# Solving the inverse's 16 by 16 diagonal blocks one to a partition, by way of DRAM

## The chip, the core and the metric

The kernel runs on one core of a Trainium2 chip. Its time is device microseconds of one execution, lower is better; a comparison takes the median of several runs on the same chip. Engines are named as in the profile: PE (TensorE matmul), PEld (its weight loads), DVE (VectorE), ACT (ScalarE), POOL (GpSimd), SP (SyncE, which here issues nearly all DMAs). All data are float32.

## What is computed

One layer of a hybrid backbone over 2048 latent tokens and 256 context tokens, 1024 channels wide. After an adaptive LayerNorm and one wide projection with w_in, branch A is a bidirectional gated delta rule with 8 heads of 128 channels, branch B a gated short convolution; both are projected, merged, projected again and added to the residual. The part that matters here is branch A's scan in chunks. With keys k, decays and write strengths beta of a chunk, the reference does

```python
m = jnp.where(tri_strict, jnp.einsum('bhncd,bhnsd->bhncs', k_beta, k) * decay, 0.0)
t_inv = lax.linalg.triangular_solve(eye + m, jnp.broadcast_to(eye, m.shape), left_side=True, lower=True)
u = t_inv @ v_beta; w = t_inv @ (k_beta * exp(g_cum))      # then, chunk after chunk:
v_new = u - w @ s; o = q_dec @ s + qk @ v_new; s = s * d + k_dec^T @ v_new
```

so each chunk, direction and head needs the inverse of a unit triangular matrix. The kernel uses chunks of 128 tokens, hence 18 chunks (16 latent, 2 context), and 128 by 128 inverses.

## The kernel before

It has three stages: the input projections (to about 1840 us of the profile), the scan with products of the two branches beside it (to about 2950 us), and the rest of those products with the output projection. In the projections, one small load (L1066) brings the 32 logit columns of w_in to 128 partitions, 8 pieces of 32 float32 (128 bytes) to a partition, 1024 pieces in all.

The scan makes 36 *visits*: 18 chunks, each for the two directions d = 0 and d = 1 in turn. A visit of all 8 heads passes through a software pipeline of four steps, so that in an iteration of the loop in `window` four visits are worked on: `v3` (the newest: loads, decays, N), `v2` (the product of queries and keys), `v1` (inverse) and `v0` (the recurrence with the state S). The order of PE's instructions is written out by hand; between them, `dense(n)` puts single matrix passes of the branch products (`pf`, L1227 to L1231), 24 in most iterations. The order on the other engines and on SP's DMA queue is made by the framework's scheduler from its own estimate of times, and at run time each of them is a queue that stands when its first instruction waits.

- `visit_decay` (L126 on) makes the decays between positions, `gcb`, on DVE (L140, eight instructions) and ACT.
- `gram` (L158 to L167) multiplies the keys of a chunk into `N`, [128, 8 heads, 128]. At the first of the two visits to a latent chunk it also keeps the product for the other direction in DRAM (`kkd`, `kqd`, by way of POOL L164); at the second it loads that (L151) and scales it with one DVE instruction (L152).
- `inv_base`, in the same iteration as N, solves the 16 by 16 blocks on N's diagonal. ACT cuts out the 32 by 32 diagonal blocks with their sign changed (`n32`, L177, four instructions); ACT and DVE bring the 16-blocks into `n16` (L180 to L182), where each of 128 partitions holds one row of a block for each head. Then 15 steps of substitution follow, with `R` starting as the identity (POOL, L185). Each has three DVE instructions: a shuffle that sends row i of each block to the other 15 partitions (L191), the product with the column i of n16 (L192), the sum into R (L193):

```python
nc.vector.stream_shuffle(rbv, R[:, :, c0:c1], [i] * 16 + [16 + i] * 16)
nc.vector.tensor_tensor(out=rbv, in0=rbv, in1=bc(n16[:, :, i:i + 1], w), op=ALU.mult)
nc.vector.tensor_tensor(out=R[:, :, c0:c1], in0=R[:, :, c0:c1], in1=rbv, op=ALU.add)
```

  Two ACT instructions (L196) spread R over the 32 columns of `r32`, and a DVE transposition of 32-blocks (L198) makes `r32t`.
- `inv_w16` (L210, copy to `w16` at L213) and `inv_d16` (L222, L224, L226), two iterations later, join 16-blocks to 32-blocks with small matmuls; `inv_w32`, `inv_d32`, `inv_w64`, `inv_d64` go on to 128.
- `st_ks` (L299, L301), `st_v` (L308), `st_o` (L319, L320) and `st_u` (L327, L332) are the recurrence; the output sums go through the callback at L1265 to L1268. The first L299 of an iteration marks its start on PE.

## Time and profile before

| | |
|---|---|
| median of 3 runs | 3305.19 us (3304.52 to 3312.04) |
| span of the profiled execution | 3301.7 us (first to last instruction) |
| PE busy | 3035.6 us, 92% |
| DVE busy | 2283.1 us, 69% |
| ACT, POOL busy | 47%, 49% |
| DMA | 481.75 MB, mean 146 GB/s |

The profile is of one execution, and for it the span is what is given; the time of the runs lies a few microseconds above it. Busy shares are averages over all three stages. Idle time is put down to the instruction that ended it ("<-").

### The profile page before, as it was taken

The numbers are of one execution on the slowest core, as the hardware profiler recorded it, in microseconds if no ns is written. First come the engines' busy times: TensorE is split into PE (matmuls) and PEld (weight loads), VectorE is DVE, ScalarE is ACT, GpSimd is POOL, SyncE is SP. The second block draws the span as 40 slices with busy tenths as digits, with TensorE's granted clock in tenths as the row PEclk, the third lists the DMA queues.
The fourth block names the chain that finished last, engine by engine and source line by source line (L and its number), as shares of the span: only waits on it lengthen the run. The fifth ranks groups of instructions, "written<-read, shape, count | busy, mean of one in ns | idle before, by whom it ended". The sixth has DMA issues, their size and how long they took to land.

```text
span 3301.7 us, 60541 instructions
## 1 busy us (share of the span) xinstructions
PE 3035.6 (92%) x22089; PEld 2484.4 (75%) x22089; DVE 2283.1 (69%) x5815; ACT 1561.9 (47%) x3453; POOL 1628.0 (49%) x1156
## 2 busy tenths in 40 slices
PE   7899999999998999999999888888889888898988
PEld 3677777788886777888878677887777777776766
DVE  7656545555646564555622678899898989978699
ACT  4664633333456555333434355555555665664321
POOL 3444557665576554666666333343343233424464
PEclk9999999999999999999999988889999989999999
DMA  5533322225564432222332654465566667667742
GB/s 210 142 99 96 95 80 87 74 64 156 173 186 136 115 93 76 64 64 65 98 108 86 214 172 150 167 196 170 174 205 212 212 216 239 219 209 241 228 146 102
DMA packets 423047, 481.75 MB, mean 146 GB/s; under 512 B 25428, under 2 KB 324949, under 8 KB 421724
## 3 DMA queue, kind: packets, MB, share of 16 engines
q1 hardware_dynamic: 413646, 470.43, 45.5%
q10 hardware_dynamic: 9102, 7.45, 0.7%
q8 instruction: 173, 2.83, 0.4%
q14 instruction: 126, 1.03, 0.1%
HBM read 341.32 MB, written 136.47 MB: 145 GB/s over the span
## 4 chain that ended last, share of the span: by engine, by line
PE 52%; DVE 25%; issue 6%; ACT 5%; DMA 5%; POOL 3%; SPq 1%; DVEq 0%; ACTq 0%; POOLq 0%
PE pd L743 13%; PE pd L744 13%; PE pd L745 13%; DVE gcb L140 3%; DVE rb L192 3%; DVE R L193 2%; POOL al L352 2%; DVE rb L191 2%; DMA gcb<-gcd 1%; PE pst L319 1%; ACT n L177 1%; POOL s L729 1%; DVE N L167 1%; PE pst L320 1%; DVE t L988 1%
## 5 line engine op out<-in xcount | busy, mean ns | idle before, releaser
L743 PE MATMUL pd<-bh,ah 128*128 128x512 f32 x2240 | 898.0, 401 | 9.8 <-ACT u L763 5.3
L745 PE MATMUL pd<-bh,al 128*128 128x512 f32 x2240 | 886.3, 396 | 0.0
L744 PE MATMUL pd<-bl,ah 128*128 128x512 f32 x2240 | 886.3, 396 | 0.0
L352 POOL TENSOR_TENSOR al<-s,ah 128x512 fp32r<-128x512 f32 x348 | 478.1, 1376 | 427.6 <-ACT ah L351 408.5
L352 POOL TENSOR_TENSOR al<-raw,ah 128x512 fp32r<-128x512 f32 x260 | 372.7, 1436 | 339.4 <-ACT ah L351 296.1
L743 PEld LDWEIGHTS pd<-bh,ah 128*128 128x128 f32 x2240 | 423.5, 189 | 107.2 <-issue 6.4
L745 PEld LDWEIGHTS pd<-bh,al 128*128 128x128 f32 x2240 | 423.5, 189 | 99.7 <-DVE al L352 0.4
L744 PEld LDWEIGHTS pd<-bl,ah 128*128 128x128 f32 x2240 | 424.0, 189 | 94.2
L351 ACT CAST ah<-s 128x512 fp32r<-128x512 f32 x352 | 215.0, 618 | 358.7 <-PE pd L744 342.8
L351 ACT CAST ah<-raw 128x512 fp32r<-128x512 f32 x264 | 162.5, 617 | 263.7 <-PE pd L744 213.8
L729 DVE TENSOR_TENSOR s<-s,raw 128x512 f32<-128x512 f32 x80 | 97.0, 1213 | 218.0 <-POOL s L729 161.5
L1231 PE MATMUL pf<-ah,wl 128*128 128x512 f32 x512 | 221.8, 433 | 6.7 <-DVE wl L352 4.6
L1227 PE MATMUL pf<-ah,wh 128*128 128x512 f32 x512 | 214.2, 419 | 12.4 <-DVE R L193 5.0
L1229 PE MATMUL pf<-al,wh 128*128 128x512 f32 x512 | 214.8, 420 | 5.9 <-POOL al L352 3.0
L352 POOL TENSOR_TENSOR wl<-wraw,wh 128x1024 fp32r<-128x1024 f32 x48 | 115.9, 2416 | 197.5 <-ACT wh L351 66.5
L192 DVE TENSOR_TENSOR rb<-rb,n 128x8 f32<-128x8 f32 (+6 forms) x540 | 200.8, 373 | 5.0
L140 DVE SCALAR_TENSOR_TENSOR gcb<-gcb,gc,mask 128x128 f32<-128x128 f32 x288 | 178.0, 623 | 9.1 <-ACT qd L137 8.1
L138 POOL TENSOR_TENSOR qd<-qd,qT 128x1024 f32<-128x1024 f32 x32 | 76.4, 2386 | 202.8 <-ACT qd L137 199.2
L193 DVE TENSOR_TENSOR R<-R,rb 128x8 f32<-128x8 f32 (+6 forms) x540 | 158.1, 294 | 5.6
L319 PE MATMUL pst<-S,qd 128*128 128x128 f32 x512 | 112.2, 304 | 33.7 <-ACT ot L1265 17.0
L768 DVE TENSOR_TENSOR u<-pd,u 128x512 f32<-128x512 f32 x80 | 55.0, 687 | 116.7 <-PE pd L745 113.6
L1005 ACT ACTIVATE t<-t 128x512 f32<-128x512 f32 (+1 forms) x112 | 67.3, 601 | 141.2 <-DVE t L990 141.2
(346 smaller groups left out, 6242.2 us busy)
## 6 DMA issues: line engine op xcount, KB each, us to landing
raw<-in_w_in SPq DMA_DIRECT2D x160, 512.0 KB, 4.0
kT<-kTd SPq DMA_DIRECT2D x36, 512.0 KB, 5.1
gcb<-gcd SPq DMA_DIRECT2D x36, 512.0 KB, 4.1
kt<-kd SPq DMA_DIRECT2D x36, 512.0 KB, 4.5
vh<-vd SPq DMA_DIRECT2D x36, 512.0 KB, 4.3
wraw<-in_w_b SPq DMA_DIRECT2D x32, 512.0 KB, 5.0
qT<-qTd SPq DMA_DIRECT2D x32, 512.0 KB, 3.9
wraw<-in_w_a SPq DMA_DIRECT2D x32, 512.0 KB, 5.2
```

Source lines behind the costliest of these rows:

```text
L140: nc.vector.scalar_tensor_tensor(out=gcb[:, h, :], in0=gcb[:, h, :], scalar=gcT[:, h:h + 1], in1=self.mask[d], op0=ALU.subtract, op1=ALU.min)
L192: nc.vector.tensor_tensor(out=rbv, in0=rbv, in1=bc(n16[:, :, i:i + 1], w), op=ALU.mult)
L193: nc.vector.tensor_tensor(out=R[:, :, c0:c1], in0=R[:, :, c0:c1], in1=rbv, op=ALU.add)
L319: nc.tensor.matmul(po[:, j, :], v["qd"][:, h, :], S[:, h, :], start=True, stop=False)
L351: self.nc.scalar.copy(out=hi, in_=src)
L352: (eng or self.nc.gpsimd).tensor_tensor(out=lo, in0=src, in1=hi.bitcast(F32), op=ALU.subtract)
L743: mm(ps, hi[:, k, :], bh, start=(first and k == 0), stop=False, skip_group_check=not first)
L744: mm(ps, hi[:, k, :], bl, start=False, stop=False, skip_group_check=not first)
L745: mm(ps, lo[:, k, :], bh, start=False, stop=(last and k == 3), skip_group_check=not first)
L1227: mm(ps, wh[:, k, :], ah, start=(k == 0), stop=False)
L1229: mm(ps, wh[:, k, :], al, start=False, stop=False)
L1231: mm(ps, wl[:, k, :], ah, start=False, stop=(k == KT - 1))
```

## The change

The base of the inverse is split into three functions, and the diagonal blocks change their layout.

- `inv_gather`, where `inv_base` was: four DMAs write N's 32 by 32 diagonal blocks to a DRAM buffer `nd` (one of four in turn), and two DMAs read from it the 16-blocks into `blk`, [64, 16, 16]: one whole block to a partition (8 heads x 8 blocks = 64). Pieces are 128 bytes for the writes and 64 for the reads, 256 and 512 of them to a DMA.
- `inv_solve`, one iteration later, behind the decays of `v3`: POOL sets the middle columns of a standing tile `X` to the identity; for each of 15 rows there is one product of column i of blk with row i of X, both broadcast (at most 64 elements on 64 partitions), and one subtraction. Two DMAs write X with its zero margins to a DRAM buffer `rd` as rows of 32, one DMA reads that back as `r32`; pieces of 128 bytes, 512 and 1024 to a DMA.
- `inv_turn`, at the start of the iteration of `inv_w16`: the DVE transposition from r32 to r32t.
- `inv_w16` takes N's own diagonal blocks, and the sign moves into the copy of `w16`.

All new DMAs are issued by SP. The constants of the old layout go away, and X and an identity are filled once ahead of the scan. (Comments are removed as well, which the diff below leaves out.)

```diff
-        i16 = pool.tile([P, 16], F32, name="i16")
...
-            nc.vector.tensor_scalar(out=t, in0=io, scalar1=idx, scalar2=None, op0=op)
-            self.tri16.append(t)
...
+        self.X = [self.g1.tile([64, 16, 48], F32, name=f"X{i}") for i in range(2)]
+        for x in self.X:
+            self.nc.gpsimd.memset(x, 0.0)
+        self.eye16 = self.g1.tile([64, 16, 16], F32, name="eye16")
+        self.nc.gpsimd.memset(self.eye16, 0.0)
+        self.nc.gpsimd.memset(self.eye16.rearrange("p r c -> p (r c)")[:, 0:256:17], 1.0)
...
-    def inv_base(self, v):
...
+    def inv_gather(self, v):
+        nd, dma = self.nd_d[v["at"] % 4], self.nc.sync.dma_start
         for g in range(4):
             s = slice(32 * g, 32 * g + 32)
-            nc.scalar.mul(out=n32[s], in_=N[s, :, s], mul=-1.0)
...
+            dma(nd[:, s, :].rearrange("h q c -> q h c"), v["N"][s, :, s])
+        v["blk"] = blk = self.g2.tile([64, 16, 16], F32, name="blk")
+        nv = nd.rearrange("h (a b r) (e c) -> (h a) b r e c", b=2, r=16, e=2)
+        for b in range(2):
+            dma(blk[32 * b:32 * b + 32], nv[:, b, :, b, :])
+
+    def inv_solve(self, v):
+        nc, g2, d, blk = self.nc, self.g2, v["d"], v["blk"]
+        v["X"] = X = self.X[v["at"] % 2]
+        nc.gpsimd.tensor_copy(out=X[:, :, 16:32], in_=self.eye16)
         for i in (range(15, 0, -1) if d == 0 else range(0, 15)):
-            c0, c1 = (i, 16) if d == 0 else (0, i + 1)
...
+            rs, cs = (slice(0, i), slice(i, 16)) if d == 0 else (slice(i + 1, 16), slice(0, i + 1))
+            xs = slice(16 + cs.start, 16 + cs.stop)
+            nr, w = rs.stop - rs.start, cs.stop - cs.start
+            pr = g2.tile([64, 64], F32, name="pr")[:, 0:nr * w].rearrange("p (r c) -> p r c", c=w)
+            nc.vector.tensor_tensor(out=pr, in0=blk[:, rs, i:i + 1].to_broadcast([64, nr, w]),
+                                    in1=X[:, i:i + 1, xs].to_broadcast([64, nr, w]), op=ALU.mult)
+            nc.vector.tensor_tensor(out=X[:, rs, xs], in0=X[:, rs, xs], in1=pr, op=ALU.subtract)
         v["r32"] = r32 = g2.tile([P, H, 32], F32, name="r32")
-        for hf in range(2):
-            nc.scalar.mul(out=r32[:, :, 16 * hf:16 * hf + 16], in_=R, mul=self.m16[hf])
-        v["r32t"] = r32t = g2.tile([P, H, 32], F32, name="r32t")
-        nc.vector.transpose(self.fl(r32t), self.fl(r32))
+        rd = self.rd_d[v["at"] % 4]
+        rv = rd.rearrange("h (a b r) c -> (h a) b r c", b=2, r=16)
+        for b in range(2):
+            nc.sync.dma_start(rv[:, b], X[32 * b:32 * b + 32, :, 16 - 16 * b:48 - 16 * b])
+        nc.sync.dma_start(r32, rd.rearrange("h p c -> p h c"))
+
+    def inv_turn(self, v):
+        v["r32t"] = r32t = self.g2.tile([P, H, 32], F32, name="r32t")
+        self.nc.vector.transpose(self.fl(r32t), self.fl(v["r32"]))
...
-                nc.tensor.matmul(wp[s, h, :], v["n32"][s, h, :], v["r32t"][s, h, :], start=True, stop=True)
+                nc.tensor.matmul(wp[s, h, :], v["N"][s, h, s], v["r32t"][s, h, :], start=True, stop=True)
...
-            nc.scalar.copy(out=v["w16"], in_=wp)
+            nc.scalar.mul(out=v["w16"], in_=wp, mul=-1.0)
...
+        self.nd_d = [dt(f"nd{i}", [H, P, 32]) for i in range(4)]
+        self.rd_d = [dt(f"rd{i}", [H, P, 32]) for i in range(4)]
...
                 if v1:
                     self.visit_load2(v1)
+                    self.inv_turn(v1)
                     self.inv_w16(v1)
...
                 if v3:
                     self.visit_decay(v3)
+                if v2:
+                    self.inv_solve(v2)
...
                     self.gram(v3, "N", v3["kT"])
-                    self.inv_base(v3)
+                    self.inv_gather(v3)
```

## Rows read from the trace of the kernel before

**Rows 1.** The page: span; busy time of each engine; DMA queue q1.

```profile
span 3301.7 us, 60541 instructions
...
PE 3035.6 (92%) x22089; PEld 2484.4 (75%) x22089; DVE 2283.1 (69%) x5815; ACT 1561.9 (47%) x3453; POOL 1628.0 (49%) x1156
...
q1 hardware_dynamic: 413646, 470.43, 45.5%
```

**Rows 2.** Windows: projections, scan, two single visits; columns in the first line.

```profile
core 0: us, PE busy (x) PEld busy (x) DVE busy (x) ACT busy (x) POOL busy (x), PEclk, DMA share, GB/s
1700.00:1800.00 100.00, 100.00 (x432) 81.04 (x431) 24.87 (x36) 40.47 (x63) 61.61 (x47) 1.00 0.34 103
1890.00:2950.00 1060.00, 925.45 (x12579) 817.34 (x12572) 941.91 (x3659) 613.32 (x1436) 388.57 (x256) 0.91 0.61 197
2307.28:2337.80 30.52, 25.94 (x377) 23.14 (x376) 28.38 (x113) 17.75 (x36) 11.03 (x8) 1.00 0.46 156
2791.54:2826.08 34.54, 29.54 (x366) 26.05 (x365) 30.19 (x114) 18.70 (x53) 12.46 (x7) 0.85 0.71 228
```

**Rows 3.** Waits of PE, 1890 to 2950: us in total, times, longest.

```profile
PE pst L299 <- DVE S L332: 17.9, 12, 4.2
PE pst L319 <- ACT ot L1265: 17.0, 13, 1.6
PE pst L299 <- DVE ot L1268: 15.7, 8, 4.3
PE pinv L222 <- ACT w L213: 15.4, 14, 2.0
PE pst L319 <- DVE ot L1268: 13.9, 6, 3.5
PE pinv L210 <- DVE r32t L198: 10.7, 10, 4.4
```

**Rows 4.** Groups by line on DVE, 1890 to 2950: busy us, mean ns | idle before.

```profile
L192 DVE TENSOR_TENSOR rb<-rb,n 128x96 f32<-128x96 f32 (+4 forms) x514 | 189.7, 369 | 4.9
...
L193 DVE TENSOR_TENSOR R<-R,rb 128x88 f32<-128x88 f32 (+4 forms) x515 | 153.5, 298 | 5.4
L191 DVE STREAM_SHUFFLE rb<-R 128x96 f32<-128x96 f32 (+7 forms) x513 | 113.2, 221 | 0.0
...
L181 DVE SCALAR_TENSOR_TENSOR n<-n,m16h,n 128x128 f32<-128x128 f32 x34 | 16.2, 477 | 21.2 <-ACT n L180 20.9
```

**Rows 5.** One line each, whole span: ns min/median/max, first and last start.

```profile
L192 DVE TENSOR_TENSOR rb<-rb,n x540: 127/226/2457, 1861.0 to 2945.9; 128x8 f32<-128x8 f32 x35, 128x32 f32<-128x32 f32 x35, 128x56 f32<-128x56 f32 x35, 128x80 f32<-128x80 f32 x35
...
L193 DVE TENSOR_TENSOR R<-R,rb x540: 154/224/2439, 1863.4 to 2946.3; 128x8 f32<-128x8 f32 x35, 128x32 f32<-128x32 f32 x35, 128x56 f32<-128x56 f32 x35, 128x80 f32<-128x80 f32 x35
```

**Rows 6.** Groups by line on ACT, 1890 to 2950.

```profile
L177 ACT ACTIVATE n<-N 32x256 f32<-32x256 f32 x136 | 56.2, 414 | 46.5 <-DVE N L152 22.7 <-DVE N L167 22.5
```

**Rows 7.** Timeline of one visit on DVE, then on PE: start us, us.

```profile
2310.51 2.16 DVE L167 SCALAR_TENSOR_TENSOR N<-gram,cc,gcb 128x128 f32<-128x128 f32 x8
...
2315.85 0.87 DVE L192 TENSOR_TENSOR rb<-rb,n 128x8 f32<-128x8 f32 x1
...
2338.24 0.27 DVE L193 TENSOR_TENSOR R<-R,rb 128x120 f32<-128x120 f32 x1
...
2337.80 1.05 PE L299 MATMUL pst<-S,kT 128*128 128x128 f32 x8
...
2340.17 0.75 PE L210 MATMUL pinv<-r32t,n 32*32 32x32 f32 x64
```

**Rows 8.** Timeline in the projections: a load of 128-byte pieces and its user.

```profile
333.56 0.37 SPq L1066 DMA_DIRECT2D tk<-in_w_in  x1
...
336.05 0.41 ACT L351 CAST wabh<-tk 128x256 fp32r<-128x256 f32 x1 [1.32 <-DMA tk<-in_w_in]
```

**Rows 9.** The tile kkd: issues (ns min/median/max) and time to landing.

```profile
L165 SPq DMA_DIRECT2D kkd<-zat x32: 319/320/320, 1966.0 to 2438.0; - x32
...
DMA to landing us min/median/max: 2.0/2.9/6.0
```

## What the change will do to the time

> **What bounds the kernel now.** I read the page first: one core, span 3301.7 us, PE busy 92% of it and DVE 69% [rows 1]. Both shares are averages over stages that differ, so the next view was the table of stretches. In the input projections (1700 to 1800 us) PE never rests, runs at its upper clock level (granted 1.00, which is 2.4 GHz) and DVE is busy a quarter of the time; in the scan (1890 to 2950 us), where the changed code lives, DVE is busy 942 of 1060 us and PE 925, and the granted clock averages 0.91 [rows 2]. So the scan, a third of the span, is held by DVE and PE together, and everything the change does happens there. It holds 34.3 visits by the count of the substitution's instructions (514 of L192, 15 to a visit, [rows 4]), 30.9 us each. The two single visits of [rows 2] show the spread: 30.5 us at clock 1.00, 34.5 us at 0.85 (a mixture of 2.4 and 1.2 GHz).
>
> PE runs a fixed order of instructions, so its idle time, 1060 - 925 = 135 us, is what a change here can win directly. The view of who waited for whom, limited to this stretch, splits it [rows 3]: the four largest waits on DVE are 17.9 + 15.7 + 13.9 + 10.7 = 58 us, the two largest on ACT 17.0 and 15.4 us. The last of the four on DVE is the base of the inverse itself: the first products of the next level (L210) stand until the transposed 32-blocks (L198) come. The others are matmuls that wait for a state update or an output sum queued on DVE behind other work. The view of groups says what that other work is: the three instructions of the substitution loop (L191 to L193) are the largest consumer of DVE [rows 4].
>
> **What is removed on DVE.** Per visit: 15 shuffles, 15 products, 15 sums and the preparation at L181, (113.2 + 189.7 + 153.5 + 16.2) / 34.3 = 13.8 us [rows 4]. (L182 is left out; it makes the gain a little larger.) The means hide something. The median product takes 226 ns and the longest 2457 [rows 5], while the mean is 369 [rows 4]: now and then one stands about as long as a large POOL instruction lasts. That excess is (369 - 226 + 298 - 224) x 15 = 3.3 us a visit, and since POOL's tensor work stays, it will fall on the new instructions or on whatever runs in their place.
>
> **What is added on DVE.** 30 instructions a visit: for row i a product of i x (16 - i) elements on 64 partitions, 15 to 64 of them, and a subtraction of the same shape. The old ones had 8 to 120 elements on 128 partitions at a median of 0.22 us, and the time follows elements on a partition, so the new ones lie below: I take 0.20, 6.0 us in all. Bounds: 6.0 without POOL's interference, 30 x 0.225 + 3.3 = 10.0 with all of it. The saving is thus 3.8 to 7.8 us a visit; I take 5, because the interference does not vanish. That is 171 us of 942: DVE at an unchanged length would be 73% busy in place of 89%. The Trainium skill (SBUF — State Buffer, "SBUF: two separate sides") says that GpSimd and a VectorE instruction with two SBUF inputs take a shared port pair by an exclusive lock for a whole instruction. The trace agrees in kind (the 2457 ns beside 226); by that rule alone the saving would be the 3.8 end, for the new products have two SBUF inputs as well.
>
> **What this gives PE.** With a sixth of DVE's work gone its queue is shorter, but the order stays, so not all of the 58 us goes: I take two thirds, -39 us (bounds 0 and -58). On ACT the four copies that cut out the 32-blocks go (L177, 56.2 us in the stretch, 1.65 a visit, [rows 6]); they stand ahead of the copy on which L222 waits 15.4 us [rows 3], and I take -12 of it (bounds 0 and -15). The 17.0 us for the output copy are untouched. The low clock costs (1 - 0.91) x 1060 = 95 us of full-speed work [rows 2]. In the stretches shown the clock is 1.00 where PE does not rest, and the lower visit is the longer one, so less idling should give some back: idle falls by 51 of 135, and I take a quarter of the 95, -24 (bounds 0 and -50).
>
> **What is added on the queues.** Nine DMAs a visit: four that put N's 32-blocks in DRAM, two that fetch the 16-blocks, two that store the solved ones, one that loads them. All are on SP, which has a single order. Each costs 0.32 us to issue [rows 9], 2.9 in all; the fetch must wait for the store before it to land, and so must the last load, and each store waits for DVE. While SP stands there, the next visit's keys, decays and the weights are queued behind it. I take +8 us (bounds 0 and +60, the latter two such waits of a visit, about 1 us each, not hidden on 30 visits). The base copy on POOL, the sign taken over by the copy after L210 and L210 reading N in place of n32 exchange one instruction for another of like shape: nothing. The constants removed and the three fills of X and the identity happen once, beside the preparation of the first visit; uncovered they would be 3 us at most.
>
> **The latency of the detour.** Before, N of a visit is ready at 2310.51 + 2.16 = 2312.7, the substitution runs from 2315.85 to 2338.5, and its products L210 start at 2340.17 [rows 7]: there are 27.5 us between N and L210. The detour has four trips through DRAM. The nearest row is a load of 1024 pieces of 128 bytes in the projections: 2.49 us from its issue to the instruction that uses it, beside another DMA [rows 8]. With that: stores 3 x 0.32 + 2.5, fetch 0.32 + 2.5, stores 0.32 + 2.5, load 2.5, transposition 0.4; 12.0 us in all. The solve has then 15.5 us for its 30 instructions, 0.52 each. Before, the 44 later ones of its 45 took 22.7 us, 0.52 each, with DVE full; back to back, 30 at about 0.25 would be 7.5. So it fits by nothing at the old pace and by 8 us at the best. A shorter visit shortens the budget with it: at 29.2 us it is 25.8. I take +10 us for visits in which it comes late (the bounds are in the rival).
>
> **The sum.** -39 - 12 - 24 + 8 + 10 = -57 us. The profiled execution's span of 3301.7 us is 3.5 below the median of the runs, 3305.2; the difference is the same after. 3305 - 57 = 3248 us. All favourable ends give -58 - 15 - 50 = -123, 3182.
>
> **Rivals.** *More than forecast.* If DVE alone set the pace, its 171 us saved would go until PE has no idle time left: -135, 3170 us. For it: DVE's 89%, and all the substitution interleaved with what PE waits for. Against: PE at 87% with its own waits on ACT. 0.15.
>
> *No change.* DVE's time is freed, but the detour uses it up: the solve ends just when L210 wants it, and PE's waits on DVE turn into waits for the load of r32. 3300 us. The equality of 0.52 and 0.52 above speaks for it. 0.12.
>
> *Slower: the detour is late.* The point is a trip of about 3.8 us: four trips more by 1.3 each eat the 5 us between a solve at 0.35 an instruction (10.5) and the 15.5 there are. Stores and loads of one buffer of 256 and 512 KB landed in 2.0 to 6.0 us with a median of 2.9 [rows 9], and ours stand on the same queue as those. At 4.4 us each L210 comes 2.6 late, on 34 visits +88 us, and the transposition that waits at DVE's head holds the rest of DVE: 3390 us. Against it: our pieces are few bytes, and DVE's other work shrinks too. 0.20.
>
> *Slower: the DMA engines fill.* There are 4 x 1024 pieces a visit. At the mean price of a packet on the queue, 45.5% x 16 x 3301.7 us / 413646 = 58 ns [rows 1], they take 4096 x 58 / 16 = 14.9 us of all engines; the late visit has 0.71 x 34.5 = 24.5 already [rows 2], together 39.4, 4.9 us over its length. On 17 such visits +83, 3388 us. Against: the load of [rows 8] had 1024 pieces done within 2.49 us, at most 39 ns each, and with that the late visit is only just full (34.4 us). 0.08. The Trainium skill (DMA: Bandwidth & Descriptors, "Specifications" and "Rules for kernel authors") gives 512 bytes as the least size for full rate, with a read-modify-write below it, and advises against many small transfers. Every piece here is 64 or 128 bytes; no row before shows such stores, so the trace neither confirms nor denies it.
>
> **How the numbers follow.** Forecast 0.45, the four rivals 0.15, 0.12, 0.20, 0.08. Between no change and a gain or loss I draw the line at 0.3%, 10 us, about what a measurement of this kernel can tell. Faster 0.60, same 0.12, slower 0.28. The likeliest case alone is 3210 to 3290. For eight in ten the range goes from 3170 to 3360: it holds the first three cases (0.72) and the mild half of the slower ones.
>
> **What the changed profile would show.** Right: DVE in the scan at 75 to 82% of a shorter stretch; products and subtractions of the solve at 0.2 us with a few at 2 us or more; PE's waits on state updates and output sums under half; granted clock above 0.91; DMA share up by 0.1 to 0.3. Wrong: PE waiting at L210, or DVE idle ahead of the transposition or of the first product of the solve, with a DMA named as the releaser; SP's waits for landings in front of the loads of keys and decays; a DMA share near 1 late in the scan. The forecast fails above all if the trips through DRAM take 4 us in place of 2.5.

## The result and the profile after

The changed kernel takes 3415.18 us (median, 3413.08 to 3419.2) where the kernel before takes 3307.98 on the same chip (3304.52 to 3312.04): 1.0326 times as long, 95% interval 1.0307 to 1.0344. It is slower by 107 us; the forecast was 3248, and the range ended at 3360.

The page of the changed kernel, the lines that answer to [rows 1]:

```profile
span 3412.5 us, 59525 instructions
...
PE 3039.0 (89%) x22089; PEld 2491.8 (73%) x22089; DVE 2143.1 (63%) x4658; ACT 1470.9 (43%) x3201; POOL 1627.8 (48%) x1159
...
q1 hardware_dynamic: 566286, 486.97, 47.9%
```

PE does the same 22089 matmuls in the same busy time as before; DVE has 140 us less. All that was lost is idle time, and the table of stretches says where. The first row is the same stretch as in [rows 2], the second goes on to the point where the changed kernel has done as many matmuls as the old one by 2950:

```profile
1890.00:2950.00 1060.00, 838.28 (x11352) 744.51 (x11351) 737.76 (x2329) 478.40 (x1057) 359.69 (x242) 0.87 0.65 191
...
1890.00:3060.00 1170.00, 928.25 (x12611) 823.07 (x12610) 814.58 (x2580) 531.76 (x1209) 389.69 (x257) 0.87 0.65 193
```

PE was busy 925 us for 12579 matmuls before and is busy 928 for 12611 now, so its idle time in the scan went from 135 to 242 us: 107 us, the whole difference. Who ended it, by the waits of PE from 1890 to 3060 (answers to [rows 3]; in all, times, longest):

```profile
PE pinv L208 <- DVE r32t L196: 137.5, 25, 10.8
PE pf L1227 <- ACT wh L349: 35.2, 4, 23.6
PE pinv L208 <- DVE pr L184: 15.4, 1, 15.4
PE pinv L208 <- DVE ms L1382: 14.2, 4, 4.6
PE pinv L285 <- ACT w L278: 11.3, 6, 3.7
PE pf L1231 <- POOL wl L350: 7.6, 3, 4.3
PE pst L297 <- DVE ot L1268: 4.1, 3, 1.9
```

The waits on state updates and output sums are nearly gone. In their place PE stands 169 us (all rows at L208 together) ahead of the first product that reads the solved blocks, where it stood 10.7 + 3.6 before, and 35 us for weights (wh) of the branch products, a wait that is not among the rows of before. The waits of DVE, and those of SP's queue, in the same stretch:

```profile
DVE QK L159 <- ACT zat L155: 65.7, 29, 3.9
DVE r32t L196 <- DMA r<-rd: 41.2, 20, 6.2
...
DVE pr L184 <- DMA blk<-nd: 18.9, 10, 3.5
```

```profile
SPq L191 <- DVE X L186: 132.5, 29, 10.0
SPq L1266 <- ACT ot L1265: 98.8, 31, 5.7
SPq L157 <- POOL zat L156: 94.2, 50, 7.4
SPq L1170 <- DVE X L186: 63.7, 11, 7.2
```

DVE, which was busy 89% of the time before, now stands for landings and for the copy of the QK product; SP stands 132 us at the store of the solved blocks until the solve's last subtraction. One visit, with the end of the one ahead of it, shows how these hang together. The timeline of DVE, then PE, then SP (start, duration, idle before and what ended it):

```profile
2297.95 0.17 DVE L186 TENSOR_TENSOR X<-X,pr 64x15 f32<-64x15 f32 x1
2298.15 2.16 DVE L159 SCALAR_TENSOR_TENSOR N<-gram,cc,gcb 128x128 f32<-128x128 f32 x8
...
2303.87 0.45 DVE L196 STREAM_TRANSPOSE r32t<-r 128x256 f32<-128x256 f32 x1 [1.50 <-DMA r<-rd]
2308.25 2.27 DVE L159 SCALAR_TENSOR_TENSOR QK<-gram,cc,gcb 128x128 f32<-128x128 f32 x8 [3.93 <-ACT zat L155]
...
2310.69 0.16 DVE L184 TENSOR_TENSOR pr<-blk,X 64x15 f32<-64x15 f32 x1
...
2320.23 7.68 DVE L132 SCALAR_TENSOR_TENSOR gcb<-gcb,gc,mask 128x128 f32<-128x128 f32 x8
...
2328.53 0.16 DVE L186 TENSOR_TENSOR X<-X,pr 64x15 f32<-64x15 f32 x1
...
2336.62 0.45 DVE L196 STREAM_TRANSPOSE r32t<-r 128x256 f32<-128x256 f32 x1 [1.69 <-DMA r<-rd]
```

```profile
2304.46 1.08 PE L208 MATMUL pinv<-r32t,N 32*32 32x32 f32 x64 [5.62 <-DVE r32t L196]
2305.47 3.21 PE L150 MATMUL gram<-qT,kT 128*128 128x128 f32 x16
...
2337.22 1.08 PE L208 MATMUL pinv<-r32t,N 32*32 32x32 f32 x64 [5.99 <-DVE r32t L196]
```

```profile
2298.15 0.85 SPq L191 DMA_DIRECT2D rd<-X  x2
...
2301.50 0.37 SPq L192 DMA_DIRECT2D r<-rd  x1
...
2304.77 0.86 SPq L172 DMA_DIRECT2D blk<-nd  x2
...
2328.71 0.85 SPq L191 DMA_DIRECT2D rd<-X  x2
2331.82 1.33 SPq L157 DMA_DIRECT2D kkd<-zat  x2
2333.25 0.38 SPq L1168 DMA_DIRECT2D gt<-gbd  x1
2333.73 0.39 SPq L192 DMA_DIRECT2D r<-rd  x1
```

Read it as a ring. PE stands 5.62 us at L208; the QK product (L150) is behind it in PE's order; DVE's scaling of that product (L159) waits 3.93 us for its copy; the solve stands behind the scaling in DVE's order, starts at 2310.69 and is cut in two by the decays, 7.68 us (in the program it stands behind them; the scheduler laid it around them). It ends at 2328.69, 18.0 us for 30 instructions. Two trips and two places in SP's order later the blocks are back, the transposition starts at 2336.62, 7.9 us after the solve, and PE has stood 5.99 us again. By this reading every late visit makes the next one late; e2_w16_late below tests that link.

### The profile page after: what moved, and what is told of

It is laid out like the page before. It is cut to its first block, busy times and chain, and to the rows that moved or that the text cites. A ratio compares the mean times of both kernels' runs of the same rounds, so it can differ in the third digit from the quotient of the medians.

```text
span 3412.5 us, 59525 instructions
## 1 busy us (share of the span) xinstructions
PE 3039.0 (89%) x22089; PEld 2491.8 (73%) x22089; DVE 2143.1 (63%) x4658; ACT 1470.9 (43%) x3201; POOL 1627.8 (48%) x1159
## 3 DMA queue, kind: packets, MB, share of 16 engines
q1 hardware_dynamic: 566286, 486.97, 47.9%
## 4 chain that ended last, share of the span: by engine, by line
PE 56%; DVE 18%; DMA 7%; issue 7%; POOL 5%; ACT 2%; SPq 1%; DVEq 0%; POOLq 0%; ACTq 0%
PE pd L745 12%; PE pd L743 12%; PE pd L744 12%; DVE gcb L132 3%; POOL al L350 2%; PE gram L150 2%; DVE X L186 2%; PE pst L306 2%; DVE pr L184 2%; DMA r<-rd 2%; PE pst L317 1%; PE pf L1231 1%; PE pf L1227 1%; PE pst L318 1%; PE pf L1229 1%
## 5 line engine op out<-in xcount | busy, mean ns | idle before, releaser
L208 PE MATMUL pinv<-r32t,N 32*32 32x32 f32 x2304 | 34.8, 222 | 176.4 <-DVE r32t L196 144.5
L208 PEld LDWEIGHTS pinv<-r32t,N 32*32 32x32 f32 x2304 | 31.1, 135 | 182.8 <-issue 175.0
L184 DVE TENSOR_TENSOR pr<-blk,X 64x15 f32<-64x15 f32 (+4 forms) x540 | 141.7, 262 | 32.4 <-DMA blk<-nd 18.9
L186 DVE TENSOR_TENSOR X<-X,pr 64x15 f32<-64x15 f32 (+4 forms) x540 | 149.7, 277 | 11.9
L1227 PEld LDWEIGHTS pf<-ah,wh 128*128 128x128 f32 x512 | 105.7, 206 | 68.2 <-ACT wh L349 38.7
L156 POOL TENSOR_TENSOR zat<-zat,cc 128x512 f32<-128x512 f32 x64 | 65.9, 1041 | 163.2 <-ACT zat L155 159.4
```

Source lines behind the costliest of these rows:

```text
L184: nc.vector.tensor_tensor(out=pr, in0=blk[:, rs, i:i + 1].to_broadcast([64, nr, w]), in1=X[:, i:i + 1, xs].to_broadcast([64, nr, w]), op=A ...
L186: nc.vector.tensor_tensor(out=X[:, rs, xs], in0=X[:, rs, xs], in1=pr, op=ALU.subtract)
L1227: mm(ps, wh[:, k, :], ah, start=(k == 0), stop=False)
```

## The experiments

Each was timed beside the kernel before, whose medians were 3303.7 to 3307.8. "w16" is PE's idle time at the first product that reads r32t, all rows summed; "wh" is its idle time put down to ACT or POOL making the weights and operands of the branch products. Both come from PE's waits, 1890 to 3060.

| run | us | ratio, 95% | w16 | wh |
|---|---|---|---|---|
| before | 3305 | | 14 | 1 |
| after | 3415 | 1.031 to 1.034 | 169 | 44 |
| e1_stale | 3405 | 1.029 to 1.034 | 43 | 127 |
| e6_free_x | 3372 | 1.018 to 1.023 | 51 | 122 |
| e7_free_all | 3346 | 1.010 to 1.016 | 26 | 121 |
| e4_double | 3475 | 1.049 to 1.055 | 125 | 124 |
| e8_pieces | 3445 | 1.040 to 1.044 | 174 | 45 |
| e9_act | 3460 | 1.043 to 1.049 | 183 | 0 |
| e2_w16_late | 3412 | 1.030 to 1.035 | 99 | 68 |
| e3_prio | 3379 | 1.021 to 1.024 | 119 | 66 |
| e12_after_w | 3411 | 1.030 to 1.036 | 181 | 8 |
| e13_both_w | 3393 | 1.025 to 1.030 | 126 | 9 |
| e10_free_w | 3334 | 1.006 to 1.012 | 44 | 28 |
| e14_early_w | 3379 | 1.020 to 1.025 | 122 | 40 |
| e18_one_w | 3373 | 1.019 to 1.023 | 118 | 33 |
| e11_before_w | 3308 | 1.000 to 1.003 | 17 | 4 |
| e16_before_early | 3309 | 1.000 to 1.003 | 16 | 1 |
| e17_shift | 3397 | 1.025 to 1.032 | 55 | 49 |
| e15_shift_early | 3359 | 1.013 to 1.019 | 62 | 20 |
| e19_half | 3303 | 0.999 to 1.002 | 49 | 12 |

**Taking the detour's waits away, one after the other.** The first run loads r32 from the buffer of the visit before.

```diff
# e1_stale
-        nc.sync.dma_start(r32, rd.rearrange("h p c -> p h c"))
+        nc.sync.dma_start(r32, self.rd_d[max(v["at"] - 1, 0) % 4].rearrange("h p c -> p h c"))
# e6_free_x: besides, the stores of the solved blocks take the other X
-            nc.sync.dma_start(rv[:, b], X[32 * b:32 * b + 32, :, 16 - 16 * b:48 - 16 * b])
+            nc.sync.dma_start(rv[:, b], self.X[(v["at"] + 1) % 2][32 * b:32 * b + 32, :, 16 - 16 * b:48 - 16 * b])
# e7_free_all: besides, the stores of N and the fetch of blk are those of the visit before
+        src, self.Nold = getattr(self, "Nold", v["N"]), v["N"]
-            dma(nd[:, s, :].rearrange("h q c -> q h c"), v["N"][s, :, s])
+            dma(nd[:, s, :].rearrange("h q c -> q h c"), src[s, :, s])
...
-        nv = nd.rearrange("h (a b r) (e c) -> (h a) b r e c", b=2, r=16, e=2)
+        nv = self.nd_d[max(v["at"] - 1, 0) % 4].rearrange("h (a b r) (e c) -> (h a) b r e c", b=2, r=16, e=2)
```

> Every instruction and every DMA stays, but r32 is loaded from the DRAM buffer that the visit before stored (so the inverse is built from another visit's blocks), and the load no longer follows this visit's solve. Theory (the solved blocks come late: PE stands at the first products of inv_w16, 170 us of waits there between 1890 and 2950): that wait goes, 3415 falls by 110 to 200 us to 3215 to 3305. Rival 1 (4096 small pieces a visit fill the DMA engines): the pieces are all there, 3380 or more. Rival 2 (other loads are held up on SP behind the new waits): the store of X still waits on SP for the solve, 3370 or more.

3405.31 us: missed, with the w16 wait three quarters gone. PE's largest wait became the weights:

```profile
PE pf L1227 <- ACT wh L349: 110.1, 12, 28.3
PE pinv L208 <- DVE r32t L196: 24.8, 3, 8.5
```

So two chains of nearly equal length held PE, and cutting one showed the other. The weights are loaded by SP, where the stores of the solved blocks still wait for the solve (L191, 91.8 us). The next run takes that wait away.

> As e1_stale, and the two stores of X take the other X tile, that of the visit before, so SP no longer stands for this visit's solve; all instructions and transfers stay (the inverse is built from another visit's blocks). New theory: the detour costs by two waits, PE for r32 at inv_w16, and SP in its one order for the end of the solve, with operand and weight loads behind it; in e1_stale the first had gone and the second took its place (PE waited 110 us for weights in 1890 to 3060). With both gone: 3250 to 3330. Rival 1 (the DMA engines fill with small pieces): nothing is taken from them, 3370 or more.

3371.83 us, missed. It is 33 us faster, and SP's wait for the solve at L191 is down to 11.6 us, yet the weights come as late as before (122 us): that wait alone did not hold them.

> As e6_free_x, and the gather stores the N of the visit before and fetches the blocks stored one visit earlier, so no DMA of the detour waits for work of the same visit; nine DMAs, 4096 pieces and 30 DVE instructions a visit stay (the inverse is again of other blocks). New theory: only waits cost, so what is left is the forecast's gain from DVE and ACT, 3225 to 3290, below the kernel before. Rival 1: 3370 or more. Rival 2 in the form that SP's nine issues (2.9 to 4 us a visit) are themselves too much: 3330 or more.

3346.04 us: the figure of rival 2, with the weights' wait whole (107.5 us, 13 times, plus 13.0 for their second part). No store of the detour waits for its own visit here. What SP stands for longest are stores that the kernel before has too (there 135.9 us for zat), and the load of r32, now most often the next DMA behind the two stores, takes SP far longer to issue: 2.0 us in the median and 4.0 at most, against 0.38 and 0.64 in the changed kernel. SP's longest waits in this run, 1890 to 2990:

```profile
SPq L157 <- POOL zat L156: 125.6, 39, 10.0
SPq L1171 <- DVE gt L1170: 82.7, 14, 11.6
```

Ahead of a wait of 17.3 us for weights at 2192.79, SP issues 27 DMAs from 2163.98 to 2186.12 almost without a pause, and the two weight loads are the last of them. Whether the longer issues or the waits for older stores make the weights late in the other cases is not separated by a run. This run's order on DVE is not that of the changed kernel either: the transposition stands ahead of N's scaling, where in the changed kernel it is behind N's scaling and vh (L299).

Between those stalls the relief of DVE is there to see. Two stretches of 100 us without one, of this run, then of before:

```profile
2000.00:2100.00 100.00, 97.91 (x1376) 87.76 (x1375) 76.97 (x283) 52.24 (x100) 41.13 (x28) 0.93 0.69 208
2200.00:2300.00 100.00, 96.36 (x1465) 87.55 (x1463) 75.67 (x273) 51.56 (x100) 40.67 (x30) 1.00 0.68 200
```

```profile
2000.00:2100.00 100.00, 86.56 (x1275) 78.04 (x1276) 88.28 (x354) 52.20 (x108) 35.34 (x26) 0.93 0.51 170
2200.00:2300.00 100.00, 89.11 (x1217) 80.15 (x1215) 91.59 (x356) 55.63 (x114) 37.11 (x27) 0.93 0.54 182
```

PE goes from 87 and 89% busy to 98 and 96%, the second time at a higher granted clock as well (1.00 beside 0.93). Two w16 products there start 25.2 us apart (2079.08 and 2104.24), which is among the shortest: up to 2492 the 17 visits in which no weight is late take 24.9 to 31.7 us, 27.1 on average, against 30.6 before in the same stretch.

**What the DMAs themselves cost.** The gather's six doubled on SP, to a buffer and a tile of their own; 4096 more pieces of 128 bytes a visit, DRAM to DRAM, issued by ACT; all nine DMAs of the detour on ACT. (Remarks behind # in this and later cuts are not in the code.)

```diff
# e4_double
+            dma(n2[:, s, :].rearrange("h q c -> q h c"), v["N"][s, :, s])      # four
...
+            dma(bk2[32 * b:32 * b + 32], nv[:, b, :, b, :])                     # two, nv now a view of n2
# e8_pieces
+        x16 = self.I["x"][0][:, 0:32].rearrange("(p k) c -> p k c", k=16)
+        for j in range(2):
+            self.nc.scalar.dma_start(self.dm_d[v["at"] % 2][j].rearrange("(p k) c -> p k c", k=16), x16)
# e9_act
-        nd, dma = self.nd_d[v["at"] % 4], self.nc.sync.dma_start
+        nd, dma = self.nd_d[v["at"] % 4], self.nc.scalar.dma_start
...
-            nc.sync.dma_start(rv[:, b], X[32 * b:32 * b + 32, :, 16 - 16 * b:48 - 16 * b])
-        nc.sync.dma_start(r32, rd.rearrange("h p c -> p h c"))
+            nc.scalar.dma_start(rv[:, b], X[32 * b:32 * b + 32, :, 16 - 16 * b:48 - 16 * b])
+        nc.scalar.dma_start(r32, rd.rearrange("h p c -> p h c"))
```

> A second copy of the six DMAs of inv_gather to buffers that nobody uses: 2048 more small pieces a visit, half as many again. Theory: they are on no path except SP's own, 3415 rises by 5 to 35 us. Rival 1 (DMA engines): half of the extra cost again, 50 us or more, 3465 and up. Rival 2 (SP): six issues and one more wait for landing a visit, 4 to 5 us on SP, 3460 and up.

> The changed kernel with two more DMAs a visit, issued by ACT without a wait, DRAM to DRAM, each 2048 pieces of 128 bytes that nobody uses: the small pieces are doubled, SP has nothing more to do. New theory: 3405 to 3440, two issues of 0.4 us on ACT. Rival 1: 4096 pieces more should cost what the first 4096 cost, 70 us or more, 3485 and up.

> The nine DMAs of the detour are issued by ACT instead of SP. New theory: SP's loads are free of the solve, but ACT's own queue now stands for N, for two landings and for the solve, and the copies that PE waits for are behind it; PE's wait at inv_w16 stays. It could go either way about the changed kernel: 3370 to 3450, with PE's waits moved from weights to ACT's copies (w16, v, output). Rival 1: no change, 3400 to 3430.

e4_double 3475.41 us, e8_pieces 3444.94, e9_act 3459.77: three misses, e8_pieces by 5 us and e9_act by 10 beyond the range of their theories, e4_double at the figure of both its rivals. e8_pieces decides between those two: twice the pieces cost 30 us when they take none of SP's time, far from the 70 that its rival asked for, so full DMA engines explain little (the pieces differ in kind, being DRAM to DRAM). Six more DMAs on SP, with 2048 pieces, cost 60, and the weights' wait went from 35 to 115 us: a place in SP's order is dearer than the bytes. On ACT the weights' wait is gone, but PE stands 29.4 us for ACT's copy of v (2.4 in the changed kernel) and 183 at w16, and it is slower still.

**Moving the work.** QK ahead of w16 on PE; a higher priority for the solve and its three DMAs, to bring them ahead of the decays.

```diff
# e2_w16_late
-                    self.inv_turn(v1)
-                    self.inv_w16(v1)
                 if v2 and v2["latent"]:
                     self.gram(v2, "QK", v2["qT"])
...
+                    self.inv_turn(v1)
+                    self.inv_w16(v1)
# e3_prio, the solve's loop to its last DMA
+        with self.tc.high_priority(1000):
```

> On PE, the product of queries and keys (or the 8 passes in its place) comes ahead of inv_turn and inv_w16 instead of behind them. Theory: the solve starts on DVE behind the scaling of that product, which stands on PE behind the late inv_w16, so the lateness feeds itself; with the order turned, 2 us of the 5.6 us wait of a visit are filled and the next solve starts sooner: 3310 to 3375. Rivals 1 and 2 (DMA engines, SP queue): no change beyond 20 us, 3395 to 3435.

> The 30 instructions of the solve and the three DMAs behind it get a higher priority with the scheduler, so that on DVE they stand ahead of the eight decay instructions (L132) instead of around them. Theory: the solve takes 8 to 11 us instead of 18, the blocks come 7 us sooner, the wait at inv_w16 falls below half: 3290 to 3350. Rivals 1 and 2: the transfers and SP's waits are as before, 3395 or more.

3412.21 and 3378.79 us, both misses; e2_w16_late is at its rivals' figure. Each cuts the ring at one place and takes 50 to 70 us from w16; the weights take some 20 of it back, and in e2_w16_late another 23 go to PE's wait for w16's copy on ACT (L220, 25.6 in place of 2.4). So the link by way of QK is there: DVE's wait for QK's copy fell from 65.7 to 10.0 us, and the solve now starts when its blocks land. But cutting it alone gives no time back: in the visit at 2302.74 the solve still takes 20.2 us, cut by 7.63 us of decays, and the transposition comes behind N's and QK's scaling. The higher priority of e3_prio is worth 36 us, though it does not take the decays out of the solve's way altogether: in the visit from 2323.26 the solve lasts 13.7 us, not the 8 to 11 that were expected.

**The weights.** Their load on ACT, in e7_free_all, in before, in after, and with both moves above:

```diff
# e10_free_w, e11_before_w, e12_after_w, e13_both_w
-        nc.sync.dma_start(raw, src[:, c0:c0 + n].rearrange("(k p) n -> p k n", p=P))
+        nc.scalar.dma_start(raw, src[:, c0:c0 + n].rearrange("(k p) n -> p k n", p=P))
```

> As e7_free_all (the detour's stores and loads take the data of earlier visits, so its output is not the reference's), and besides the load of the branch weights (tile wraw) is issued by ScalarE instead of SyncE. Theory: what is left in e7_free_all is TensorE standing 107.5 us for ScalarE's copies of weights whose loads wait in SyncE's order behind stores that wait for VectorE and GpSimd; off that queue those waits fall under 30 us, and of the 3346 us some 60 to 100 go: 3240 to 3290 us, below the 3305 of before, so the solve along the free axis does give about what it was to give once no ordered wait stands in its way. Rival 1: the weights are late because the DMA engines are slow or ScalarE gets to the copy late, not because of SyncE's order: the waits for the weights stay above 80 us and the time above 3330 us. Rival 2: ScalarE's own queue now holds the load back behind its other work: the waits move to other tiles of ScalarE and the time is 3310 us or more.

> The kernel before with the weights' load alone issued by ScalarE; everything is computed. A control for e10_free_w. Theory: SyncE's order does not hold TensorE up before the change (no wait for weights is among the rows of its waits above 12 us), so 3290 to 3320 us, within 0.5% of before. Rival: the move is a gain by itself, under 3280 us, and then what e10_free_w gains says nothing of the change.

> The changed kernel with the weights' load issued by ScalarE; everything is computed. Theory: TensorE's 35 us of waits for weights go, but its 170 us at the products of w16 stay, since the solve still starts behind the scaling of the second triangular product and is still cut by the decays: 3370 to 3410 us. Rival: the weights were the hidden main cause, and without them the loop comes early enough: under 3340 us.

> The changed kernel with three moves in the order of work and nothing left out: the solve and its three transfers ahead of the decays in VectorE's order, the products of w16 behind the triangular product QK on TensorE, and the weights' load on ScalarE. Theory: each takes a part of the loop away (the solve starts earlier, QK's product no longer waits behind w16, the weights no longer wait in SyncE's order): TensorE's waits at w16 fall under 60 us and those for weights under 25 us, 3290 to 3345 us, about the time before. Rival: the tail of two transfers behind the solve is the same length wherever the solve stands, so that w16 still waits 90 us or more: 3350 to 3390 us.

The control e11_before_w is unchanged (3308.07), and e12_after_w at the upper end of its range (3410.98): off SP the weights are in time (8 us), and w16 takes it all. e13_both_w, 3393.43, went to the rival (w16 126 us; the time is 3 us above its range). e10_free_w, 3333.51, missed, as rival 2 has it: the weights' wait fell to zero, but the wait for ACT's copy ahead of L286 rose from 6.7 to 26.5 us, and 24 came in for operands, which SP still loads. Two more runs tried e7_free_all with the weights in time by other means, with a control on before:

```diff
# e14_early_w, e16_before_early: load and split apart, the load one unit ahead
-                        if k == 2 and m < 7:
-                            w = self.load_w(W, (m + 1) * P)
+                        if k == 2 and raw is not None:
+                            u = 8 * jn + m + 2
+                            w, raw = self.split_w(raw), self.load_w(*units[u]) if u < len(units) else None
# e18_one_w: loads as they were, into a tile that nobody reads, with one buffer in place of two
-        raw = self.wp.tile([P, KT, n], F32, name="wraw", bufs=2)
+        raw = self.wp.tile([P, KT, n], F32, name="wst" if self.wst is None else "wraw", bufs=1)
...
-        return self.split_w(raw, n)
+        self.wst = self.wst or raw; return self.split_w(self.wst, n)
```

> As e7_free_all (the detour takes the data of earlier visits, so its output is not the reference's), and besides each branch weight is loaded one unit of eight matrix passes earlier, still by SyncE, its split into two parts staying where it was. Theory: e7_free_all's 107.5 us of TensorE waits for weights are loads held back in SyncE's order by stores that wait for VectorE and GpSimd, and a load issued a unit ahead is back in time whatever stands before it: these waits fall under 25 us and the visits go at about the 25.2 us that e7_free_all's undisturbed visits take: 3235 to 3290 us. Rival 1: the load only moves the queue's blockage to another load (operands, keys, values) and the time stays 3320 us or more. Rival 2: the weights' waits stay, because ScalarE or the DMA engines and not the issue are late: 3330 us or more with the same row in the waits.

> The kernel before with each branch weight loaded one unit earlier; everything is computed. A control. Theory: no row of weights above 1 us stands among TensorE's waits before, so 3295 to 3320 us, no change. Rival: a gain of 1% or more by itself, under 3275 us, so that what e14_early_w gains is not owed to the queue of the changed kernel.

> As e7_free_all (the detour takes the data of earlier visits), and besides ScalarE and GpSimd split the first branch weight again and again, from a tile that stays, while every weight is still loaded by SyncE at its old place into a tile that nobody reads; the output is not the reference's. Theory: SyncE's late loads are what is left in e7_free_all: TensorE's waits for weights go from 107.5 us to near nothing, the visits take 25 to 27 us in the first half of the scan, and the time is 3235 to 3290 us. Rival: the same delay of SyncE makes the next thing late (the operands, the keys or the values), so TensorE's waits move and the time stays 3315 us or more.

The control did nothing (3309.33). Both others missed (3379.07 and 3372.75), though the waits for weights are gone (what "wh" shows are operands): w16 is back at some 120 us with r32 long in its tile, as DVE waited for its landing only twice in each, 10.9 and 9.5 us in all. DVE's timeline in e18_one_w says why:

```profile
2316.97 0.61 DVE L331 SCALAR_TENSOR_TENSOR S<-S,d,pst 128x128 f32<-128x128 f32 x2 [3.51 <-PE pst L326]
2317.49 0.16 DVE L185 TENSOR_TENSOR pr<-blk,X 64x15 f32<-64x15 f32 x1
...
2336.14 2.14 DVE L300 SCALAR_TENSOR_TENSOR vh<-pst,ngam,vh 128x128 f32<-128x128 f32 x8
2338.21 0.42 DVE L197 STREAM_TRANSPOSE r32t<-r 128x256 f32<-128x256 f32 x1
```

The scheduler had laid DVE's work in another order: the solve starts behind a state update that waits for PE, and the transposition is the last of the visit, behind N's scaling and vh; PE waited 5.38 us for it at 2338.78. In e7_free_all's timeline (2322 to 2343) the solve starts ahead of the state updates, and the transposition ahead of N's scaling and vh. An edit to the weights' load alone went with another order on DVE. In that order PE stands two thirds as long at w16 as in the changed kernel, though no DMA of the detour waits for work of its own visit; in the changed kernel, too, the transposition comes behind N's scaling and vh.

**Both causes in a kernel that computes everything.** The chain of inverse steps half a visit later on PE, on top of e3_prio, and then the weights a unit early as well:

```diff
# e17_shift (and e15_shift_early, with the early load)
+                if v0:
+                    self.inv_w64(v0)          # head of the next visit, ahead of QK
...
+                if v0:
+                    self.inv_d64(v0)          # ahead of the decays
...
+                    self.st_v(v0, 1)
+                if v1:
+                    self.inv_turn(v1)
+                    self.inv_w16(v1)          # d16, w32 and d32 follow
```

> The changed kernel with the solve and its three transfers ahead of the decays, and the whole inversion chain from the transposition on moved later by some half a visit: w16 behind the products of v, the two last steps (w64, d64) at the head of the next visit, so the blocks have some 12 us more to come back; everything is computed. Theory: the waits at w16 (93.7 us and more in e3_prio) fall under 40 us, those for weights stay at 60 to 110 us as in e1_stale and e7_free_all: 3330 to 3375 us. Rival: the solve depends on DVE's order and comes later by as much as w16 does, so the wait stays above 80 us and the time is 3370 us or more.

> As e17_shift, and each branch weight loaded one unit earlier, so both causes are taken at once and everything is computed. Theory: with the blocks and the weights both in time the relief of VectorE shows: 3250 to 3310 us, at or below before. Rival: what TensorE waits for moves on to other loads behind the detour in SyncE's order (operands, stored products), or to the copies behind w64 and d64 that now stand close together: 3330 us or more.

3396.99 and 3358.91 us, both misses. w16 fell to 55 to 62 us. Shorter waits did not become time one for one: e17_shift has 52 us less of them than e3_prio in the rows of PE's waits (158 and 210 us) and is 18 us slower, which no run explains. In e15_shift_early the two halves of the scan differ, by the count of w16's products (64 to a visit) in stretches of 520 and 530 us (their busy time and count, then granted clock, DMA share, GB/s); before, e15_shift_early, then the last experiment, e19_half:

```profile
1900.00:2420.00 520.00, 13.55 (x1088) 0.90 0.52 173
2420.00:2950.00 530.00, 14.79 (x1148) 0.92 0.69 221
```

```profile
1900.00:2420.00 520.00, 13.79 (x1152) 0.94 0.69 202
2420.00:2950.00 530.00, 13.86 (x960) 0.84 0.68 205
```

```profile
1900.00:2420.00 520.00, 13.84 (x1152) 0.93 0.69 202
2420.00:2950.00 530.00, 15.20 (x1088) 0.88 0.67 215
```

17 and 17.9 visits before, 18 and 15 in e15_shift_early: the first half gains a visit in 520 us, the second, where N and QK come from DRAM and the DMA share was 0.69 before any detour, loses three. The share is no higher there with the detour (0.68), and the clock is lower; why the second half loses is not shown. So the old substitution was put back for the second half (blk gets one buffer, and two POOL fills take the place of the copy of the identity):

```diff
# e19_half
-                    self.inv_gather(v3)
+                    (self.inv_base if v3["again"] else self.inv_gather)(v3)
```

> Everything is computed. The 20 visits of the scan that form their own triangular products take the changed solve with the order of e15_shift_early (solve ahead of the decays, chain shifted by half a visit, weights a unit early); the 16 that load stored products take the substitution of the kernel before, in the place it had there. Theory: the first half keeps e15_shift_early's gain (its first 19 visits took some 35 us less than those before), the second half goes at the 30 us a visit of before, since it has no detour and its DMA engines are as before: 3255 to 3300 us, below before. Rival 1: the second half is slow for another reason (the weights' early loads or the order on SyncE), so the time is 3310 to 3360 us. Rival 2: the gain of the first half is given back where the two forms meet and in fillers left for the end: 3300 to 3315 us.

3303.01 us beside 3303.91 (ratio 1.0003, 0.9991 to 1.0015): the changed solve at no cost, and no gain, as rival 2 said. The first half kept its visit (18 in 520 us); the second has 17, and where the forms meet PE stands twice, 19.8 and 11.8 us (of 36.9 put down to the old substitution in all):

```profile
2459.54 1.08 PE L248 MATMUL pinv<-r32t,N 32*32 32x32 f32 x64 [19.79 <-DVE rb L229]
```

DVE's timeline shows it: the transposition of the last changed visit (2458.99) stands behind the whole old substitution of the visit after it.

## Why the prediction was wrong

- **DVE's work: the instructions right, the saving too large.** Products and subtractions have medians of 200 and 201 ns (0.20 was taken) and means of 262 and 277 (page of after), 15 x 0.539 = 8.1 us a visit, inside the bounds of 6.0 and 10.0. By that 13.8 - 8.1 = 5.7 us would be saved. But DVE's busy time in the scan fell from 942 to 815 us, 127 and not 171, or 3.7 us a visit where 5 was taken: durations of rows overlap (before, all groups of DVE in the scan add up to 1124 us, with 942 busy), so 13.8 us from group rows is more than DVE's time. The excess of the means over the medians, (62 + 76) x 15 = 2.1 us, agrees in kind with the port lock that the prediction cited from the Trainium skill (SBUF — State Buffer, "SBUF: two separate sides"); the longest subtraction took 2414 ns.
- **PE's old waits, -39 and -12: right but for one, and worthless.** Three of the four DVE waits of [rows 3], 47.5 us, fell to 6.3, and L220's for its copy from 15.4 to 2.4. In e7_free_all, where PE stands only 26 us at w16, the three are at 9.8 us, so this is DVE's relief and not only PE standing elsewhere first. But the fourth, PE's wait for the transposed blocks, was counted among those that shrink, and with its other rows it went from 14 to 169 us.
- **The clock, -24: wrong sign.** The granted clock in the scan fell from 0.91 to 0.87, with PE idle 21% of 1170 us in place of 13% of 1060.
- **The latency of the detour, +10: the step that failed.** The trips were about what was taken. In the visit before the one shown, the last subtraction ends at 2298.12, the load of r32 is issued at 2301.50 and the transposition starts at 2303.87: 5.75 us, with 2.5 us from the end of the stores' issue (2299.0) to the load and 2.4 for the load. What was wrong is the budget: 27.5 us from N to L210, of which 15.5 were left for the solve, as if DVE took it up when the blocks land. In the visit shown N is ready at 2300.31 and L208 starts at 2337.22, 36.9 us later. The solve starts 10.4 us after N where 6.3 was taken, since DVE's order puts it behind QK's scaling, which hangs on PE's wait for the blocks of the visit ahead. It lasts 18.0 us for 15.5, since the decays (7.68 us) cut it. From its end to L208 it is 8.5 us for 5.7, as SP issues the load only 4.2 us after the stores, behind kkd and gt. Of these 9.4 us too many PE stands for 6.0; it comes to L208 itself 30.9 us after N. That is the rival "the detour is late" (0.20). Its 3390 us is near the measured time by luck, for its own reason did not hold: a trip of 3.8 us was not needed. Of the 169 us at w16, DVE itself stood only 41 for the landing of r32. Moving the solve or w16 takes 50 to 114 us from this wait (e2, e3, e17), and e14 and e18 show some 120 us of the same wait with hardly a landing waited for, so DVE's order looks like the larger part. What is shown for the time: with no transfer of the detour waited for in its own visit (e7), 69 of the 107 us are gone, though in another order on DVE.
- **SP's queue, +8: mis-sized.** PE's waits for weights are 44 us in the changed kernel, within the bound of 60, and 121 to 127 us in e1, e6 and e7, where less time is lost at w16. e10_free_w and e12_after_w show that it is the place on SP: on ACT's queue the same loads are in time. The reason given, that the detour's DMAs wait for landings and for DVE, is at most a part: in e7 they wait for nothing of their own visit, and the weights are as late. The 0.32 us for an issue did not hold everywhere either (the load of r32: 0.38 us in the changed kernel, 2.0 in e7).
- **DMA engines full (0.08): hardly.** Twice the pieces cost 30 us, and the share rose by 0.04, not by 0.1 to 0.3. The price of 58 ns a packet was too high for these: by the lines of q1 on the two pages, the 152640 packets that came in took (47.9% x 3412.5 - 45.5% x 3301.7) x 16 us, 13.9 ns each.
- **"More than forecast": not reached.** In e7_free_all's undisturbed visits PE is 96 to 98% busy at some 27 us a visit, and 3346 less its waits for weights would be about 3225, if nothing came in their place. Something did in every run that tried: the best with blocks of other visits is 3334 (e10_free_w); with everything computed it is 3359 with the changed solve in all visits and 3303 with it in 20 of 36. Whether an order exists that does better stays open, and so does what holds the last 28 us of e10_free_w.

## What to carry to other kernels

Work that is moved to a longer way with less engine time pays only where its result has slack; count that from the moment the engine's order reaches the work, not from when its data land, and look whether what stands ahead of it waits, through other engines, for the same result of the round before. A DMA costs the in-order queue that issues it, by its issue and by its wait for a producer, so list the loads behind it before pricing its bytes. When one wait is removed and the time stays, read the waits again: a second chain of the same length may lie under the first, and a scheduler that orders by its own times can turn one such edit into several. A sum of durations by group is not busy time where instructions overlap; take the difference of busy times when the trace after is there.

## What the runs showed of the hardware

Small pieces were cheap for the DMA engines and dear for the queue that issues them. 4096 more of 128 bytes a visit, from DRAM to DRAM, cost 30 us over 36 visits, 0.8 us each, and the pieces of the detour took 13.9 ns of an engine each. The Trainium skill (DMA: Bandwidth & Descriptors, "Rules for kernel authors") advises against many small transfers; here six DMAs in SP's order, with half as many pieces, cost twice as much. The load of r32, 1024 pieces, took SP 0.38 us to issue (median) in the changed kernel and 2.0 us in e7_free_all, where it does not wait for the two stores ahead of it to land; why is not shown.
